# Where the operands of the products lie in the on-chip memory

## The chip, the cores and the metric

The kernel runs on one core of one Trainium2 chip. The metric is the device time of one execution in microseconds. The time before is the median of three runs, 3551.01 us (3549.99 to 3552.76).

## The reference

512 tokens of 1024 features go through two blocks of two layers each. A layer of the first block is: a SwiGLU feed-forward layer with 2816 hidden features, a token mixer (stick-breaking attention, gated delta rule and short convolution side by side), a second feed-forward layer, and a gated embedding; a layer norm follows each of the four. The two layers of the second block are attention layers: the first has three groups of windowed and dilated attention in eight heads, the second has grouped-query attention; both read 256 memory tokens as well, gate their heads, and add an output projection to x. Everything is float32. In short:

```
for i in range(DEPTH):
    x = layer_norm(ALPHA * x + 0.5 * swiglu(x, ffn_w_in[i, 0], ffn_w_out[i, 0]), ...)
    x = layer_norm(ALPHA * x + token_mix(x, ...), ...)
    x = layer_norm(ALPHA * x + 0.5 * swiglu(x, ffn_w_in[i, 1], ffn_w_out[i, 1]), ...)
    x = layer_norm(ALPHA * x + sigmoid(x @ w_gate + b) * (p[i] @ w_proj), ...)
# then, twice:  x = x + (attention heads * silu(gate)) @ w_out
```

## The kernel before, in words

Features lie on the 128 partitions, tokens along the free dimension, so a feature tile of all tokens is 128x512. Every dense product is made of three float32r products. `weight` (L144) brings a piece of a weight, [128, 1024] or [128, 768], into a staging tile `wst`, ScalarE casts it to its high part `whi` (L153), and VectorE or GpSimd takes the difference as the low part `wlo` (L154). The activations are split in the same way (`split`, L175): `xh` and `xl` are the parts of x, `hh` and `hl` those of the hidden features of a feed-forward layer, `mxh` and `mxl` those of the mixed heads, `Yh` and `Yl` those of the gated heads of the second block, `mem_p` those of the memory tokens. One step is then low weight times high activation, high weight times low activation, and high times high. Each TensorE product is a weight load (128 columns of the stationary operand) and a matmul that streams the moving operand, 512 or 256 columns wide.

In the first block the weights are stationary and the activations move, in `mm3` (L190), `mm3_side` and `gmm3`: results `pgu` (w_in of a feed-forward layer), `pfo` (w_out), `pmx` (projections of the mixer), `pmo` (its output), `pg` and `ppp` (the gated embedding). In the second block `mm3k` (L1151) does them. For `p_in` (projections to heads) and `p_mkv` (keys and values of the memory tokens) the activations are stationary and the weights move; for `p_gate` and `p_out` it is as in the first block. The attention itself (`att_p`, `att_o`, transposes `att_T`, `nh_t`) and the delta rule are plain float32 products between working tiles, no weights in them.

The order of the work is the order of the code, with engines waiting for each other by semaphores; the next weights are brought in while the present ones are used (two staging tiles, five pairs of parts). The change touches none of this; it touches where tiles lie.

The pools are laid one behind another along each partition in the order in which they are opened, and each tile's place is rounded up to 32 bytes. A scratch area of 16384 bytes and four constants of 32 bytes come first. Then come `const` (L116 to L128: 512 + 512 + 32 + 512 + 512 + 512 + 32 bytes), `ph` (`xh`, `xl`, 16384 bytes each), `pst` (two `wst`), `pwh` and `pwl` (five `whi`, five `wlo`, 4096 bytes each), then x or, in the second block, `mem_all`, then the small tiles of a region and its working tiles. This adds up to the following places. A tile of weights or activations within these starts a multiple of 512 bytes further on, so the remainder by 128 holds for all of them.

| tile | byte | remainder by 128 |
|---|---|---|
| `xh` / `xl` | 19136 / 35520 | 64 |
| `wst`, `whi`, `wlo` (first of each) | 51904, 60096, 80576 | 64 |
| x, `mem_all` | 101056 | 64 |
| working tiles of the first block (`hh`, `hl`, `mxh`, `mxl`, `mem_p` of its last layer, ...) | 128960 + 2048 n | 64 |
| working tiles of the second block (`Yh`, `Yl` from 157824, `mem_p` from 126080 and 145536, q, k, v) | | 0 |

So before the change the parts of weights and activations have the same remainder in all products but two: `p_out`, and `p_mkv` in its second use (at some 3190 us).

Of the kernel before, what the change touches and what calls it, by code (L numbers as in the profile page):

```python
# [31 lines left out]


class Kern:
    def __init__(self, ctx, tc, ins, outs):
        self.tc, self.nc, self.i, self.o = tc, tc.nc, ins, outs
        self.ctx = ctx
        pool = lambda n, b, **k: ctx.enter_context(tc.tile_pool(name=n, bufs=b, **k))
        self.const = pool("const", 1)
        self.ph = pool("ph", 1)  # L40
        self.pst = pool("pst", 2)
        self.pwh = pool("pwh", 5)
        self.pwl = pool("pwl", 5)
        self.pd = pool("pd", 4, space=PSUM)
        self.pm = pool("pm", 4, space=PSUM)
        self.fence = None
        self.clock = 0
        self.looked = []
        self.table(SILU)
        self.consts()  # L50

    @contextmanager
    def region(self, **sizes):
        """Working tiles of one stretch of the program."""
# [8 lines left out]
    # ---------------------------------------------------------------- tiles  # L63
# [27 lines left out]
    def table(self, name):  # L91
        """Load the activation table of what follows, once what needed the one before is done."""
        load = self.nc.scalar.preload_act_table_set(name)
        for i in self.looked:
            self.behind([load], i)
        self.looked.clear()
        return load

    def behind(self, later, first):
        """Issue order only: the instructions later go after first on their engine."""  # L100
# [5 lines left out]
    def chain(self, seq):  # L106
        """One accumulation group over several parts of a bank: the first product opens it, the last one closes it."""
        self.behind(seq[1:], seq[0])
        for i in seq[1:-1]:
            self.behind(seq[-1:], i)  # L110

    def consts(self):
# [6 lines left out]
        self.ones = c.tile([128, 1], F, name="ones")  # L119
        nc.vector.memset(self.ones, 1.0)  # L120
        self.m128 = c.tile([128, 128], F, name="m128")
        nc.vector.memset(self.m128, 1.0 / 128)
        self.mean_r = c.tile([128, 128], FR, name="mean_r")
        nc.vector.tensor_copy(self.mean_r, self.m128)
        self.ones128 = c.tile([128, 128], F, name="ones128")
        nc.vector.memset(self.ones128, 1.0)
        self.qeps = c.tile([128, 1], F, name="qeps")
        nc.vector.memset(self.qeps, 128.0 * EPS * EPS)  # L128
# [16 lines left out]
    # ---------------------------------------------------------------- weights  # L145
    def weight(self, src, n, eng=None):
        """One piece of a weight, [128, n] in DRAM, as two float32r parts whose sum is exact."""
# [11 lines left out]
    def unit(self, src, eng=None, spare=False):  # L159
        """The exact parts of a weight [128, 1024], by tiles [128, 128]; spare: held in working tiles."""  # L160
# [18 lines left out]
    # ---------------------------------------------------------------- products  # L179
    def turn(self, out, a):  # L180
        """out = a transposed."""
# [3 lines left out]
    def mm(self, out, lhsT, rhs, start, stop):  # L185
        """A product, and its columns on the tensor engine's clock."""
# [3 lines left out]
    def mm3(self, out, pairs):  # L190
        """out += sum over pairs of (stationary hi, lo), (moving hi, lo), small products first."""
# [9 lines left out]
    def mm3_side(self, groups):  # L201
        """Several products that share their moving operands, (out, stationary parts, moving parts), one pair of each
        before the next: they start while the last moving parts are still being made."""
# [9 lines left out]
    def gmm3(self, out, pairs, step=3):  # L213
        """mm3 as a generator that yields every few products."""
# [11 lines left out]
    # ---------------------------------------------------------------- statistics  # L226
    def rsqrt(self, y, v, n):
        """y = v ** -0.5, elementwise on [128, n]."""
# [14 lines left out]
    def bcast(self, out, cols):  # L243
        """out[p, j, t] = cols[t, j] for the 128 tokens t of cols [128, n], by two exact products each."""
# [13 lines left out]
class LN:  # L258
    """Layer norm over the features of y [128, 8, 512] (feature k * 128 + p), in place, fed tile by tile."""
# [6 lines left out]
    def add(self, f, ps, tk, scale):  # L266
        """y[:, f, tk] = y[:, f, tk] + scale * ps - c, c a per-token shift near the mean; f = 0 comes first."""
# [37 lines left out]
    def begin(self, tk):  # L305
        """Statistics of the tokens tk, y less its mean."""
# [28 lines left out]
    def end(self, tk, xh=None, xl=None, lead=True):  # L335
        """Normalise the tokens tk; y becomes the layer norm, xh + xl its exact parts."""
# [19 lines left out]
def ffn(K, l, j, x, xh, xl, ln, aside=None, load=None):  # L356
    """x += 0.5 / ALPHA * swiglu(x), through ln."""
# [23 lines left out]
    if load:  # L381
        # the first tokens arrive between the first weights
# [52 lines left out]
def weave(K, chains, dense):  # L435
    """Issue the tensor engine's work of chains, each of which yields how long its next step has to wait (columns), the
    first that is ready first, and of dense, which never waits for long, in between."""
# [24 lines left out]
# waits, in columns of the tensor engine  # L462
# [10 lines left out]
def mixer(K, l, xh, xl, ln):  # L473
    """x += token_mix(x) / ALPHA, through ln."""
# [22 lines left out]
    def b3(col, n=128):  # L497
        """[128, m] -> [128, m, n], repeated along the last axis"""
        return col.unsqueeze(2).to_broadcast([128, col.shape[1], n])

    def rep(m):
        """[128, n] -> [128, NH, n], repeated along the heads"""
        return m.unsqueeze(1).to_broadcast([128, NH, m.shape[1]])

    # q, k, v: projection, causal convolution, silu; features on the partitions
    qt = [K.t2((128, NH, 128), name="gq") for _ in range(4)]
    kt = [K.t2((128, NH, 128), name="gk") for _ in range(4)]
    # x is but xh + xl now; its place serves for others
# [3 lines left out]
    def conv(j, p, tk, before=None):  # L512
        """The tokens tk of the unit j, p [128, tk] in PSUM, after the three tokens before."""
# [16 lines left out]
    # values of the stick breaking attention and gates a, b, by token tile  # L530
# [82 lines left out]
def _mixer_heads(K, l, mixed, out, places, xh, xl, ab, sv, qt, kt, vt, a_log, dt_b, norm_w, sc_w, unit, gproj, b3, rep, silus, pre):  # L613
# [26 lines left out]
    def norms(ts):  # L640
        """Keys by token for the tiles ts, and the coefficients that their norms give."""
# [34 lines left out]
    def decays(t):  # L676
        """exp of the differences of the sums of log decays within the chunks, and of those sums."""
# [10 lines left out]
    def start():  # L688
        pre[0] = K.table(LOG)

        # decays and gates, [128 tokens, tile * head]
# [52 lines left out]
    def piece(t):  # L744
# [12 lines left out]
        # U = (I + N^T)^-T by doubling blocks  # L757
# [99 lines left out]
    def tail(t, po, qsq):  # L857
        """Gated rms norm; the norm of q enters through its eps."""
# [33 lines left out]
    def stick(pair):  # L892
        """Stick breaking attention of two heads, scores with the keys on the partitions: for each head keys 0 in a tile
        and keys 1 and 3 in another, for both keys 2 in a third."""
# [65 lines left out]
    def gate():  # L960
        """silu of the gate z of the gated delta net, by token tile."""
# [13 lines left out]
    def short(i):  # L975
        """Short convolution, half i."""
# [38 lines left out]
def ple(K, l, x, xh, xl, ln, rms=None, aside=None):  # L1015
    """x += sigmoid(x @ w_gate + b) * (p @ w_proj) / ALPHA, through ln."""
# [28 lines left out]
    def some(fs, W, tk):  # L1045
        """Part of the output for the tokens tk; the first products go tile by tile of x."""
# [47 lines left out]
# -------------------------------------------------------------------- second block  # L1094
#
# Token n = 128 * c + i of the second block is token 4 * i + c of the sequence: a tile of 128 tokens is
# one residue class modulo 4, so the two dilated groups stay within a tile.
# [8 lines left out]
def by_class(a):  # L1106
    """[128, 512] in sequence order -> [128, 4, 128] in the second block's order."""
# [3 lines left out]
def by_time(a):  # L1111
    """[128, 512] in the second block's order -> [128, 128, 4] in sequence order."""
# [3 lines left out]
def row_sums(K, q, tk):  # L1116
    """[128 tokens, tiles] in PSUM: column sums of q over the tokens tk."""
# [8 lines left out]
def row_rsqrt(K, st, n, eps, name, fence=False):  # L1126
    """[128, tokens] in PSUM, the same on every partition: (st / n + eps) ** -0.5."""
# [23 lines left out]
def mm3k(K, out, pairs, step=6):  # L1151
    """Like mm3, but done with each pair before the next; yields every few products."""
# [10 lines left out]
def norm_heads(K, ps, nh, gain, rope, dst):  # L1163
    """Rms norm by head of ps [128 tokens, nh, 128], rotated, then with the features on the partitions in dst."""
# [36 lines left out]
class Pieces:  # L1201
    """[128, 8, 256] held as four tiles [128, 2, 256]."""
# [16 lines left out]
def mem_norm(K, R):  # L1219
    """R [128, 256], on every partition: the inverse rms of the memory tokens."""  # L1220
# [13 lines left out]
def mem_parts(K, l, R, tiles):  # L1234
    """The norm of the memory tokens in exact parts, held in tiles [128, 2, 256]."""
# [10 lines left out]
def mem_kv(K, l, hh, hl, mk, mv, eng=None, which=(0, 1)):  # L1246
    """Keys [128, head, 256] and values [128, tile, 4 * 128] of the memory tokens."""
# [15 lines left out]
class RMS:  # L1263
    """Rms norm over the features, x(f) [128, 512] being feature tile f, into xh + xl in the second block's order."""
# [5 lines left out]
    def from_time(self, tk):  # L1270
        """Sums of squares of the tokens tk, sequence order."""
# [14 lines left out]
    def scale_time(self, tk, after=None):  # L1286
        """The normalised tokens tk, still in sequence order."""
# [21 lines left out]
    def add(self, f, ps, tk):  # L1309
        """x += ps for the tokens tk, in the second block's order, and the sum of squares."""  # L1310
# [34 lines left out]
class Head:  # L1345
    """One head of attention: scores(c) gives the scores of the queries of tile c, pieces of nk * 128 columns in PSUM,
    each with a mask to add or None; values(kt) the values of key tile kt, a list by query tile where each sees
    another; done(o) takes the result [128 features, 512] in PSUM."""
# [6 lines left out]
    def soft(self, cp):  # L1355
        """Softmax of the queries of two tiles."""
# [26 lines left out]
    def mix(self, cp):  # L1383
        """Their values."""
# [29 lines left out]
def attend(heads, ahead=0):  # L1414
    """The heads in turn; softmaxes run ahead of the values by so many pairs of tiles."""
# [21 lines left out]
def project(K, xh, xl, W, n, evac):  # L1437
    """Projection by tiles of 128 tokens: evac(c, PSUM [128, n])."""
# [13 lines left out]
class Slab:  # L1452
    """Feature tiles [128, 512] kept two to a tile."""
# [23 lines left out]
def gates(K, l, es, xh, xl, O, Y):  # L1477
    """y = o * silu(gate), in exact parts, for the feature tiles es."""
# [443 lines left out]
```

## Time and profile before

| | |
|---|---|
| median of the runs | 3551.01 us |
| span of the profiled execution, from the first to the last instruction | 3551.5 us (0.5 us above the median; the page gives no time around it) |
| TensorE, matmuls | 3410.5 us busy, 96%, 17964 of them |
| TensorE, weight loads | 2898.7 us busy, 82% |
| VectorE / ScalarE / GpSimd | 1944.7 us (55%) / 1248.1 us (35%) / 721.7 us (20%) |
| mean granted clock of TensorE | 0.975 |
| DMA | 294.40 MB, mean 83 GB/s |

A matmul's busy time contains its way through the array, so that matmuls overlap in the records; what one of them costs in a dense stretch is the distance between two starts, read from the timeline.

### The profile page before, as it was taken

To read this page: it belongs to the slowest core of one execution; us is meant where nothing else is said; L and a number is where in the kernel's file an instruction comes from. 1 tells how busy PE (TensorE), PEld (TensorE's weight loads), DVE (VectorE), ACT (ScalarE), POOL (GpSimd) and SP (SyncE) were. 2 spreads that over 40 slices of the span, in tenths; PEclk is the share of its full clock that TensorE was granted. 3 is DMA by queue.
4 is the path that set the end of the run, shared out by engine and by line. 5 is a ranking of instruction groups with operands and counts; after the bars stand their busy time and mean duration, and the time that the engine had idled before them with its cause. 6 is when DMAs were issued, how large, how long until landed. Compare 5 with 4: busy or idle time off the path is not lost. (4 is left out here: it accounts for less than half of the span.)

```text
span 3551.5 us, 46067 instructions
## 1 busy us (share of the span) xinstructions
PE 3410.5 (96%) x17964; PEld 2898.7 (82%) x17964; DVE 1944.7 (55%) x4167; ACT 1248.1 (35%) x2104; POOL 721.7 (20%) x560
## 2 busy tenths in 40 slices
PE   8999899999999799998999999987999999999998
PEld 7888887788887788888978888876888888887777
DVE  3333665663334733346565533368767767549665
ACT  3322435332223332224353322244333333334332
POOL 0002313450012500123234200234122212111100
PEclk9999999999999899999999999997999999999999
DMA  4323211123232133232111232323322222233112
GB/s 154 109 86 98 78 37 54 36 79 103 98 92 87 48 107 98 86 92 69 45 39 54 86 99 92 94 95 111 102 75 74 75 85 73 75 127 118 56 46 79
DMA packets 91657, 294.40 MB, mean 83 GB/s; under 512 B 14256, under 2 KB 16944, under 8 KB 91312
## 3 DMA queue, kind: packets, MB, share of 16 engines
q1 hardware_dynamic: 91440, 291.47, 26.0%
q8 instruction: 141, 2.31, 0.3%
q14 instruction: 76, 0.62, 0.1%
HBM read 283.96 MB, written 7.47 MB: 82 GB/s over the span
## 5 line engine op out<-in xcount | busy, mean ns | idle before, releaser
L154 DVE TENSOR_TENSOR wlo<-wst,whi 128x1024 fp32r<-128x1024 f32 (+1 forms) x403 | 479.8, 1191 | 728.2 <-ACT whi L153 725.1
L153 ACT CAST whi<-wst 128x1024 fp32r<-128x1024 f32 (+1 forms) x520 | 531.3, 1024 | 874.0 <-issue 276.0
L188 PE MATMUL pgu<-xh,wlo 128*128 128x512 f32 (+1 forms) x1504 | 568.4, 378 | 0.2 <-ACT silu L374 0.2
L188 PE MATMUL pgu<-xl,whi 128*128 128x512 f32 (+1 forms) x1504 | 564.5, 378 | 0.0
L154 POOL TENSOR_TENSOR wlo<-wst,whi 128x1024 fp32r<-128x1024 f32 x117 | 280.4, 2401 | 609.2 <-ACT whi L153 597.6
L188 PE MATMUL pgu<-xh,whi 128*128 128x512 f32 (+1 forms) x1504 | 384.9, 379 | 11.4 <-ACT xh L176 8.9
L188 PEld LDWEIGHTS pgu<-xh,whi 128*128 128x128 f32 x1504 | 287.0, 191 | 62.8 <-ACT xh L176 8.9
L188 PEld LDWEIGHTS pgu<-xh,wlo 128*128 128x128 f32 x1504 | 287.3, 191 | 51.8 <-ACT silu L374 0.6
L188 PEld LDWEIGHTS pgu<-xl,whi 128*128 128x128 f32 x1504 | 284.7, 190 | 51.8 <-DVE xl L177 0.8
L1157 PE MATMUL p_in<-whi,xl 128*128 128x512 f32 (+1 forms) x800 | 304.9, 383 | 5.9 <-DVE xl L1307 4.5
L1157 PE MATMUL p_in<-wlo,xh 128*128 128x512 f32 (+1 forms) x800 | 305.7, 382 | 0.0
L1157 PE MATMUL p_in<-whi,xh 128*128 128x512 f32 (+1 forms) x800 | 305.2, 382 | 0.0
L285 POOL TENSOR_TENSOR x<-x,ln_c 128x256 f32<-128x256 f32 (+1 forms) x84 | 96.2, 1178 | 969.4 <-ACT ln_c L282 969.4
L188 PE MATMUL pfo<-hl,whi 128*128 128x512 f32 (+1 forms) x792 | 282.7, 366 | 0.0
L188 PE MATMUL pfo<-hh,wlo 128*128 128x512 f32 (+1 forms) x792 | 282.3, 365 | 0.0
L375 DVE TENSOR_TENSOR silu<-silu,pgu 128x512 f32<-128x512 f32 (+1 forms) x94 | 61.4, 653 | 224.9 <-PE pgu L188 190.7
L188 PE MATMUL pmx<-xl,whi 128*128 128x512 f32 (+1 forms) x480 | 182.4, 383 | 0.0
L1157 PEld LDWEIGHTS p_in<-whi,xl 128*128 128x128 f32 x800 | 151.6, 189 | 34.0 <-DVE xl L1307 4.7
L188 PE MATMUL pmx<-xh,wlo 128*128 128x512 f32 (+1 forms) x480 | 179.2, 374 | 0.0
L1157 PEld LDWEIGHTS p_in<-wlo,xh 128*128 128x128 f32 x800 | 151.6, 190 | 27.7 <-issue 2.6
L1157 PEld LDWEIGHTS p_in<-whi,xh 128*128 128x128 f32 x800 | 151.5, 189 | 27.5 <-issue 2.4
L188 PEld LDWEIGHTS pfo<-hh,wlo 128*128 128x128 f32 x792 | 149.4, 189 | 24.2
(376 smaller groups left out, 6463.1 us busy)
## 6 DMA issues: line engine op xcount, KB each, us to landing
wst<-in_ffn_w_in SPq DMA_DIRECT2D x176, 512.0 KB, 3.4
wst<-in_ffn_w_out SPq DMA_DIRECT2D x64, 512.0 KB, 3.5
wst<-in_wa_qk SPq DMA_DIRECT2D x48, 512.0 KB, 3.4
wst<-in_ffn_w_out SPq DMA_DIRECT2D x32, 384.0 KB, 3.2
wst<-in_mix_w_qkv SPq DMA_DIRECT2D x24, 512.0 KB, 3.5
wst<-in_wa_v SPq DMA_DIRECT2D x24, 512.0 KB, 3.4
wst<-in_w_gate SPq DMA_DIRECT2D x24, 512.0 KB, 3.2
wst<-in_w_out SPq DMA_DIRECT2D x32, 384.0 KB, 3.1
```

The source lines that it names most:

```text
L153: nc.scalar.copy(hi, st)
L154: sub = (eng or nc.vector).tensor_sub(lo, st, hi.bitcast(F))
L188: return self.nc.tensor.matmul(out, lhsT=lhsT, rhs=rhs, start=start, stop=stop)
L285: nc.gpsimd.tensor_sub(self.y[:, k, tk], self.y[:, k, tk], c)
L375: nc.vector.tensor_mul(s, s, ps[1])
L1157: K.nc.tensor.matmul(out, lhsT=w, rhs=x, start=(j == 0), stop=(j == n - 1))
```

## The change

Two small tiles of 64 bytes are put into pools of their own, one between the staging tiles and the parts of the weights, one behind these. The constants are laid out anew: the two single columns share a tile of 128 bytes, and `m128` is no tile any more but another view of `mean_r`, which is now made from `ones128`. One small tile of the second block is made 64 bytes longer. Comments and docstrings are dropped too, so line numbers move.

```diff
+LINE = 32
...
         self.pst = pool("pst", 2)
+        self.off = pool("off", 1)
+        nc = self.nc
+        self.words = self.off.tile([128, LINE // 2], F, name="words")
+        nc.vector.memset(self.words, 0.0)
         self.pwh = pool("pwh", 5)
         self.pwl = pool("pwl", 5)
+        self.off2 = pool("off2", 1)
+        self.words2 = self.off2.tile([128, LINE // 2], F, name="words2")
+        nc.vector.memset(self.words2, 0.0)
...
-        self.ones = c.tile([128, 1], F, name="ones")
+        both = c.tile([128, LINE], F, name="both")
+        self.ones, self.qeps = both[:, 0:1], both[:, 1:2]
         nc.vector.memset(self.ones, 1.0)
-        self.m128 = c.tile([128, 128], F, name="m128")
-        nc.vector.memset(self.m128, 1.0 / 128)
-        self.mean_r = c.tile([128, 128], FR, name="mean_r")
-        nc.vector.tensor_copy(self.mean_r, self.m128)
+        nc.vector.memset(self.qeps, 128.0 * EPS * EPS)
         self.ones128 = c.tile([128, 128], F, name="ones128")
         nc.vector.memset(self.ones128, 1.0)
-        self.qeps = c.tile([128, 1], F, name="qeps")
-        nc.vector.memset(self.qeps, 128.0 * EPS * EPS)
+        self.mean_r = c.tile([128, 128], FR, name="mean_r")
+        nc.vector.tensor_scalar(self.mean_r, self.ones128, 1.0 / 128, None, op0=OP.mult)
+        self.m128 = self.mean_r.bitcast(F)
...
-            g = load_small(K, ins["norm_g"][1], (128, KD), "rmsg")
+            g = K.sm.tile([128, KD + LINE // 2], F, name="rmsg", tag="rmsg", bufs=1)[:, :KD]
+            nc.sync.dma_start(out=g, in_=ins["norm_g"][1])
```

By the same adding up the places become: `xh` 18688, `xl` 35072, first `wst` 51456 (all remainder 0 by 128); first `whi` 59712, first `wlo` 80192 (remainder 64); x and `mem_all` 100736, working tiles of the first block from 128640, `Yh` and `Yl` from 157568 (all remainder 0).

## Rows read from the trace of the kernel before

**Rows 1.** The page's first part: busy us (share of the span) xinstructions.

```profile
PE 3410.5 (96%) x17964; PEld 2898.7 (82%) x17964; DVE 1944.7 (55%) x4167; ACT 1248.1 (35%) x2104; POOL 721.7 (20%) x560
```

**Rows 2.** Groups of matmuls, 512 columns: shape, xcount | busy us, mean ns | idle before.

```profile
L188 PE MATMUL pgu<-xh,wlo 128*128 128x512 f32 x1312 | 511.6, 390 | 0.2 <-ACT silu L374 0.2
L1157 PE MATMUL p_in<-wlo,xh 128*128 128x512 f32 x672 | 268.8, 401 | 0.0
...
L188 PE MATMUL pfo<-hl,whi 128*128 128x512 f32 x616 | 239.7, 389 | 0.0
L188 PE MATMUL pmx<-xl,whi 128*128 128x512 f32 x352 | 145.0, 412 | 0.0
...
L1157 PE MATMUL p_gate<-xh,wlo 128*128 128x512 f32 x192 | 77.3, 403 | 0.0
```

**Rows 3.** The same view, products of 256 columns.

```profile
L188 PE MATMUL pmo<-mxl,whi 128*128 128x256 f32 x256 | 66.9, 295 | 3.7 <-DVE mxl L177 3.7
...
L188 PE MATMUL pgu<-xh,wlo 128*128 128x256 f32 x192 | 56.9, 299 | 0.0
L188 PE MATMUL pg<-xh,wlo 128*128 128x256 f32 x192 | 53.7, 292 | 1.8 <-ACT sig L1055 1.8
L188 PE MATMUL pfo<-hl,whi 128*128 128x256 f32 x176 | 43.0, 285 | 0.0
L188 PE MATMUL pmx<-xh,wlo 128*128 128x256 f32 x128 | 37.9, 299 | 0.0
L1157 PE MATMUL p_in<-wlo,xh 128*128 128x256 f32 x128 | 36.8, 288 | 0.0
```

**Rows 4.** Timeline, feed-forward w_in, 512 columns, twelve products apart: start us, us, what.

```profile
99.81 0.39 PE L188 MATMUL pgu<-xl,whi 128*128 128x512 f32 x1
...
102.53 0.39 PE L188 MATMUL pgu<-xl,whi 128*128 128x512 f32 x1
```

**Rows 5.** Timeline, feed-forward w_out, 256 columns, fifteen products apart.

```profile
358.12 0.28 PE L188 MATMUL pfo<-hh,wlo 128*128 128x256 f32 x1
...
359.92 0.28 PE L188 MATMUL pfo<-hl,whi 128*128 128x256 f32 x1
```

**Rows 6.** Timeline, output projection of the second block, 512 columns, sixteen apart.

```profile
3462.63 0.40 PE L1157 MATMUL p_out<-Yl,whi 128*128 128x512 f32 x1
...
3466.36 0.40 PE L1157 MATMUL p_out<-Yh,whi 128*128 128x512 f32 x1
```

**Rows 7.** Timeline, output projection of the second block, 256 columns, nine apart.

```profile
3522.01 0.28 PE L1157 MATMUL p_out<-Yh,whi 128*128 128x256 f32 x1
...
3523.03 0.28 PE L1157 MATMUL p_out<-Yh,whi 128*128 128x256 f32 x1
```

**Rows 8.** Timeline, second p_mkv, keys: fifteen products between these two.

```profile
3191.82 0.63 PE L1157 MATMUL p_mkv<-whi,mem_p 128*128 128x512 f32 x2
...
3195.32 0.63 PE L1157 MATMUL p_mkv<-whi,mem_p 128*128 128x512 f32 x2
```

**Rows 9.** Timeline, second p_mkv, values: sixteen products between these two.

```profile
3207.69 0.39 PE L1157 MATMUL p_mkv<-wlo,mem_p 128*128 128x512 f32 x1
...
3211.36 0.39 PE L1157 MATMUL p_mkv<-wlo,mem_p 128*128 128x512 f32 x1
```

**Rows 10.** Timeline, mixer output, 256 columns, five products apart.

```profile
743.93 0.41 PE L188 MATMUL pmo<-mxl,whi 128*128 128x256 f32 x1
...
745.00 1.91 PE L188 MATMUL pmo<-mxh,whi 128*128 128x256 f32 x8
```

**Rows 11.** Windows, that stretch: busy us by engine, PEclk, DMA share, GB/s.

```profile
744.00:746.00 2.00, 2.00 (x11) 2.00 (x11) 2.00 (x5) 0.42 (x1) 0.00 (x0) 0.50 0.63 229
```

**Rows 12.** VectorE groups that take the low parts: xcount | busy us, mean ns.

```profile
L154 DVE TENSOR_TENSOR wlo<-wst,whi 128x1024 fp32r<-128x1024 f32 x339 | 417.9, 1233 | 494.3 <-ACT whi L153 491.3 <-PE p_in L1157 0.9 <-PE p_gate L1157 0.4
L177 DVE TENSOR_TENSOR hl<-silu,hh 128x512 fp32r<-128x512 f32 x82 | 56.2, 686 | 4.1 <-ACT hh L176 4.1
...
L177 DVE TENSOR_TENSOR Yl<-gated,Yh 128x512 fp32r<-128x512 f32 x12 | 8.2, 684 | 0.7 <-ACT Yh L176 0.7
```

## The prediction, made before the changed kernel was seen

> **What bounds the kernel now.** I read the page's first part, then the groups of matmuls by shape, and then the timeline of single stretches. The first part says that TensorE's matmuls are busy 96% of the span, VectorE 55%, ScalarE 35%, GpSimd 20% [rows 1]. So nearly all of the time is the distance from one matmul to the next, and a change that only moves addresses can act at one place of weight: that distance. It has to be read from the timeline, because the mean of a row (390 ns for a product of 512 columns [rows 2]) contains the way through the array.
>
> In the feed-forward layer, with all weights at hand, twelve products of 512 columns take 102.53 - 99.81 = 2.72 us, 226.7 ns each [rows 4]. Products of 256 columns take (359.92 - 358.12) / 15 = 120.0 ns [rows 5]. What would they take without any loss? At the lower granted clock of 0.5 (1.2 GHz of the two levels), 256 columns take (745.00 - 743.93) / 5 = 214 ns [rows 10, 11], which is a column per cycle: 256 / 1.2 = 213.3. A column per cycle at 2.4 GHz would be 213.3 ns for 512 and 106.7 ns for 256. So at the full clock each product loses 13.4 ns (32 cycles) in either width, and at the half clock it loses none. Something is read too slowly only when TensorE runs fast; it is neither a semaphore nor a DMA, as the two starts lie in stretches without a gap.
>
> **A comparison that lies in the trace already.** Of all products with weights, two have their operands where the change puts them all, one at a multiple of 128 bytes and the other 64 bytes past one: `p_out`, whose `Yh` and `Yl` have remainder 0 and whose weights have 64, and the second `p_mkv`, with `mem_p` at 0 and weights at 64. They keep other distances than the rest:
> - `p_out`, 256 columns: (3523.03 - 3522.01) / 9 = 113.3 ns [rows 7] against 120.0. That is a gain of 6.7 ns, 16 cycles.
> - `p_out`, 512 columns: (3466.36 - 3462.63) / 16 = 233.1 ns [rows 6] against 226.7. That is a loss of 6.4 ns, again 16 cycles.
> - the second `p_mkv`, 512 columns, weights moving and activations stationary: (3195.32 - 3191.82) / 15 = 233.3 ns for the keys [rows 8], and (3211.36 - 3207.69) / 16 = 229.4 ns for the values [rows 9].
>
> So with unlike remainders the narrow products run faster and the wide ones slower, whichever of the operands moves. The wide ones know two rhythms, 233 and 229; each was kept over a whole stretch, so which one a stretch has seems to depend on how it was entered.
>
> **The change part by part.**
> - *Products of 512 columns in the two feed-forward stages.* `pgu` has 3 x 1312 = 3936 and `pfo` 3 x 616 = 1848 of them, 5784 in all; of the three products of a step one row stands [rows 2], the others have the same count. They form long dense streams like those of rows 4. Bounds for each: +2.7 ns (229.4) and +6.6 ns (233.3). I take the upper one, as `p_out` has the same roles (weights stationary at 64, activations moving at 0) and it showed 233: 5784 x 6.6 = +38 us.
> - *Products of 512 columns mixed with short ones.* `p_in` 3 x 672 = 2016, `p_gate` 3 x 192 = 576, `pmx` 3 x 352 = 1056, together 3648. Their means are 401 to 412 ns against 390 [rows 2]: attention and delta-rule products between them disturb the rhythm and they pay some of the loss today. Bounds 0 and +6.6 ns; I take half, +3.3: 3648 x 3.3 = +12 us. The few left (`ppp`, the first `p_mkv`) are under 300 products, below 2 us.
> - *Products of 256 columns.* Six kinds, three products each: 3 x (256 + 192 + 192 + 176 + 128 + 128) = 3216 [rows 3]. Each goes from 120.0 to 113.3: 3216 x -6.7 = -21.5 us. Bounds: -21.5 and 0 (the gain is lost where a narrow product waits for its operands anyway or runs at the half clock).
> - *What stays.* `p_out` and the second `p_mkv` keep unlike remainders. The float32 products of the attention have both operands among working tiles, which move together, and contain no weights. Value projections of the first block and the spare weights of its last gated embedding hold their weights in working tiles and move together with `xh` and `xl`: no change.
> - *VectorE, ScalarE, GpSimd.* Their operands move too. Taking a low part of 512 columns lasts 686 ns with all operands at 64 and 684 ns with all at 0 [rows 12]; unlike ones, as `wst` and `whi` become, no row here shows apart from others. If each `wlo` of 1233 ns became 10% longer or shorter, 339 x 0.12 = 42 us would come or go on an engine that has 45% of the span free [rows 1, 12], and the next weights are split while TensorE works on the present ones; without that cover it would be 42 us either way. Taken: 0, by the two equal rows.
> - *The constants.* One memset and a copy less, two memsets of 16 columns and a multiply more, on VectorE at the start, while the first weights are on their way: 0. No instruction is moved past a queue, and no wait is added.
>
> Sum: 38 + 12 - 21.5 = +28.5 us on the profiled execution's 3551.5, which is 0.5 us above the median; on the median this gives 3579.5, say 3580 us. The lower end, 229.4 throughout and nothing in mixed stretches, is 5784 x 2.7 - 21.5 = -6 us. The upper end, +6.6 everywhere and the full gain on narrow products, is 9432 x 6.6 - 21.5 = +41 us; with narrow products that gain nothing, +62 us.
>
> **The rivals.**
> 1. *The other rhythm.* The streams settle at 229 and not at 233. For it: the values of `p_mkv` did [rows 9]. Against it: these have the roles exchanged, and the stretches of `p_out` keep 233 [rows 6]. Time: 3551 - 6 to 3551 + 6, about 3549; the sign of its difference is open.
> 2. *The wide products gain as the narrow ones do.* If operands in different halves of 128 bytes never meet, a dense stream would lose 16 cycles less in either width: 9432 x -6.7 - 21.5 = -85 us, 3466 us. For it: the narrow products [rows 7], and that 32 cycles lost at like remainders are 16 there. Against it: no product of 512 columns in the trace does it, and those with unlike remainders do the opposite [rows 6, 8].
> 3. *Addresses are not the cause.* `p_out` and `p_mkv` differ from the rest in more than the remainder (another stage, other pools). Then nothing changes: 3551 us. Against it: `p_in`, in the same block and written by the same function but with like remainders, has means that lie with the first block's (288 ns at 256 columns, against 285 to 299 there [rows 3]), while every stretch shown with unlike remainders deviates [rows 6 to 9]. The Trainium skill, "SBUF — State Buffer", section "Who interferes with whom", has this as its rule: "PE and ACT never wait on anyone", with two independent read ports for the moving operand and the weight load. By that rule the time stays at 3551. The trace does not agree with it as it stands, since equal products keep 120.0 and 113.3 ns [rows 5, 7] and neither is a column per cycle.
>
> **How the numbers follow.** A difference over 0.2%, 7 us, can be told from no change. Forecast (slower, +7 to +62 us): 0.62. First rival: 0.15, of which two thirds within 0.2%, the rest shared. Second: 0.13. Third: 0.10. Slower: 0.62 + 0.03 = 0.65. Within 0.2%: 0.10 + 0.10 = 0.20. Faster: 0.13 + 0.02 = 0.15. The predicted time is 3580 us. The range is to hold the forecast, the first and the third rival: 3540 to 3603. The upper end is 52 us above the median, between the two upper sums. The second rival is left out, as is what lies above. The forecast's own range is 3558 to 3603.
>
> **What would show it right or wrong.** In the changed kernel's timeline the distance of `pgu` and `pfo` of 512 columns should be 233 ns and that of 256 columns 113 ns; `p_out` should stay at 233 and 113. TensorE's idle time and the counts of its groups should stay as they are, and the difference should lie mostly in the four feed-forward stages. A distance of 229 there makes the first rival right, one of 220 the second, one of 227 the third. If VectorE's or ScalarE's rows grow by a tenth and TensorE begins to wait for `wlo`, my zero for them was wrong.

## The result and the profile after

The changed kernel takes 3585.01 us (median of four runs, 3576.35 to 3587.90) against 3551.89 us (median of four runs of the kernel before): a ratio of 1.0089, 95% interval 1.0077 to 1.0101. It is slower by 33 us; 28.5 us were forecast.

First the page's first part after the change, which answers to [rows 1].

```profile
PE 3443.6 (96%) x17964; PEld 2892.9 (81%) x17964; DVE 1940.9 (54%) x4168; ACT 1243.9 (35%) x2104; POOL 721.8 (20%) x560
```

The span went from 3551.5 to 3585.3 us, by 33.8 us, and the matmuls' busy time by 3443.6 - 3410.5 = 33.1 us. TensorE's idle time is the same (141.0 and 141.7 us), the counts too, and the other engines are no busier. So the time lies between matmul and matmul. Which of them, the groups by shape say (xcount | busy us, mean ns of one), in answer to [rows 2, 3]:

```profile
L196 PE MATMUL pgu<-xh,wlo 128*128 128x512 f32 x1312 | 519.1, 396 | 0.2 <-ACT silu L382 0.2
L1165 PE MATMUL p_in<-wlo,xh 128*128 128x512 f32 x672 | 269.4, 401 | 0.0
L196 PE MATMUL pfo<-hl,whi 128*128 128x512 f32 x616 | 241.2, 392 | 0.0
...
L196 PE MATMUL pgu<-xh,wlo 128*128 128x256 f32 x192 | 55.5, 292 | 0.0
...
L196 PE MATMUL pfo<-hl,whi 128*128 128x256 f32 x176 | 42.3, 281 | 0.0
```

`pgu` of 512 columns grew by 6 ns, `pfo` by 3, `p_in` by none; the narrow ones of `pgu` and `pfo` shrank by 7 and 4. These means contain the way through the array, so the distance between starts decides. In the timeline (start us, us, what) this is the feed-forward w_in, sixteen products from the first row to the last, as [rows 4]:

```profile
99.22 0.40 PE L196 MATMUL pgu<-xl,whi 128*128 128x512 f32 x1
...
102.95 0.40 PE L196 MATMUL pgu<-xl,whi 128*128 128x512 f32 x1
```

It gives 3.73 / 16 = 233.1 ns, the forecast's rhythm. Feed-forward w_out of 512 columns (27 products, 22 of them in the first row) and of 256 columns (15 products, as [rows 5]), and the output projection of 256 columns (11 products, as [rows 7]):

```profile
345.80 5.20 PE L196 MATMUL pfo<-hh,whi 128*128 128x512 f32 x22
...
351.98 0.39 PE L196 MATMUL pfo<-hl,whi 128*128 128x512 f32 x1
...
366.88 0.28 PE L196 MATMUL pfo<-hh,wlo 128*128 128x256 f32 x1
...
368.65 0.28 PE L196 MATMUL pfo<-hl,whi 128*128 128x256 f32 x1
...
3556.80 0.28 PE L1165 MATMUL p_out<-Yh,wlo 128*128 128x256 f32 x1
...
3558.10 0.28 PE L1165 MATMUL p_out<-Yh,whi 128*128 128x256 f32 x1
```

These are 6.18 / 27 = 228.9 ns, 1.77 / 15 = 118.0 ns and 1.30 / 11 = 118.2 ns. None of the three is what I wrote down: `pfo` of 512 columns runs in the rhythm of the first rival, its narrow products gain 2 ns and not 6.7, and `p_out`, which was to stay at 113.3 ns, got slower. The remainders by 128 are as the change set them in all of these, so the remainder by 128 cannot be the whole rule.

Taking the places modulo 256 instead of 128 shows a candidate. In the changed kernel the weights lie 64 bytes past a multiple of 256, `xh` and `xl` at a multiple, but `hh`, `hl`, `Yh`, `Yl` 128 bytes past one. So the distance moving minus stationary is -64 for `pgu` and +64 for `pfo`. In the kernel before it was 0 for both, and -64 for `p_out`, which now has +64.

### The profile page after: what moved, and what is told of

It reads as the page before. It is cut to its first block, busy times and chain, and to the rows that moved or that the text cites. A ratio compares the mean times of both kernels' runs of the same rounds, so it can differ in the third digit from the quotient of the medians.

```text
span 3585.3 us, 46068 instructions
## 1 busy us (share of the span) xinstructions
PE 3443.6 (96%) x17964; PEld 2892.9 (81%) x17964; DVE 1940.9 (54%) x4168; ACT 1243.9 (35%) x2104; POOL 721.8 (20%) x560
## 4 chain that ended last, share of the span: by engine, by line
PE 85%; DVE 9%; issue 3%; ACT 2%; DMA 1%; POOL 1%; SPq 0%; DVEq 0%; ACTq 0%; POOLq 0%
PE pgu L196 27%; PE p_in L1165 14%; PE pfo L196 13%; PE pmx L196 5%; PE p_gate L1165 4%; PE p_out L1165 3%; PE pmo L196 2%; PE att_o L1412 2%; PE p_mkv L1165 1%; PE att_T L191 1%; PE pg L196 1%; PE pU L196 1%; PE pZ L196 1%; PE nh_t L191 1%; PE att_p L1577 1%
## 5 line engine op out<-in xcount | busy, mean ns | idle before, releaser
L196 PE MATMUL pgu<-xl,whi 128*128 128x512 f32 (+1 forms) x1504 | 573.1, 384 | 0.1
L196 PEld LDWEIGHTS pfo<-hh,wlo 128*128 128x128 f32 x792 | 148.7, 188 | 25.6
```

What stands on the lines that cost most here:

```text
L196: return self.nc.tensor.matmul(out, lhsT=lhsT, rhs=rhs, start=start, stop=stop)
```

## The experiments

The three layouts below that are whole kernels are compared with 3554.35 us, the median of thirteen runs of the kernel before that were made beside them. The theory, called D in the expectations: the distance moving minus stationary, modulo 256 and with its sign, sets the rhythm. Rival E: like or unlike remainders by 128, with the entry into a stretch choosing between 229 and 233. Rival A: each operand's own alignment.

**A sweep by 32 bytes.** A program of products alone, between one stationary and one moving tile whose starts have the same remainder by 256:

```diff
+order = [(w, s, m) for w in (512, 256) for s in range(8) for m in range(8)]
+for turn, seq in (("x", order), ("y", order[::-1])):
+    for w, s, m in seq:
+        p = pd.tile([128, 512], F, ...)
+        for k in range(40):
+            nc.tensor.matmul(p[:, :w], lhsT=W[:, 8 * s + k % 8 * 128:8 * s + k % 8 * 128 + 128],
+                             rhs=M[:, 8 * m + k % 4 * 512:8 * m + k % 4 * 512 + w], start=(k == 0), stop=(k == 39))
```

> This kernel has nothing of the model: it makes 40 float32r products in a row, weight load and matmul, for each pair of byte offsets of the stationary and the moving operand (0 to 224 by 32), 512 and 256 columns wide, all pairs once forward and once backward. Theory D (what counts is the distance moving minus stationary, taken modulo 256, with its sign): the distance between two starts is the same along each diagonal of the table; 0 gives 226.7 and 120.0 ns (512 and 256 columns), -64 gives 233.3 and 113.3 ns, +64 gives 229 and 117.8 ns, 128 is open. Rival A (each operand's own alignment counts): rows or columns of the table are alike, not diagonals. Rival E (like or unlike remainders by 128 count, and how a stretch was entered picks the rhythm): 0 and 128 are alike, 226.7 and 120.0; +64 and -64 are alike, each 229 or 233 by chance, and differ between the forward and the backward pass.

Measured, from the starts of the last 25 products of each 40, in ns; 16 stretches stand behind each number (eight pairs of offsets, twice):

```
distance      0      32     64     96     128    160    192    224
512 columns   226.7  233.3  228.9  233.3  232.9  234.4  233.3  233.3
256 columns   120.0  117.4  117.8  120.0  118.7  117.7  116.1  118.3
```

At 512 columns the 16 stretches of a distance agree within 0.3 ns, those of 128 within 1.2; with one operand kept in its place and the other moved, the spacing goes through all these values. So theory D holds there and rival A falls. Of rival E the remainder by 128 falls: 0 and 128 are not alike, +64 and -64 (192) are not alike. Its other half, the entry, does not fall: at 256 columns the 16 stretches at 192 keep either 113.3 ns (six of them) or 117.8 ns (ten), where theory D expected 113.3 for all.

**All remainders alike, at a multiple of 256.** The changed kernel without the two small tiles:

```diff
-        self.off = pool("off", 1)
-        self.words = self.off.tile([128, LINE // 2], F, name="words")
-        nc.vector.memset(self.words, 0.0)
...
-        self.off2 = pool("off2", 1)
-        self.words2 = self.off2.tile([128, LINE // 2], F, name="words2")
-        nc.vector.memset(self.words2, 0.0)
```

> The changed kernel without its two small tiles ahead of and behind the parts of the weights: activations stay at a multiple of 128, the parts of the weights come to one too, and every distance is 0 modulo 256, that of the output projection of the second block and of the second memory projection too. Theory D: 226.7 and 120.0 ns everywhere, 3551 us plus p_out's change (288 x -6.6 + 576 x 6.7 ns = +2 us), 3550 to 3556 us. Rival A (the activations' move to a multiple of 128 costs the time): it stays near 3585 us. Rival E: as theory D.

Measured: 3555.64 us against 3554.35, a ratio of 1.0004, interval 0.9995 to 1.0014. In its timeline the feed-forward w_in (eleven products between the rows) and the output projection of 256 columns (ten products):

```profile
99.19 0.39 PE L190 MATMUL pgu<-xl,whi 128*128 128x512 f32 x1
...
101.68 1.52 PE L190 MATMUL pgu<-xh,whi 128*128 128x512 f32 x6
...
3520.93 0.28 PE L1159 MATMUL p_out<-Yl,whi 128*128 128x256 f32 x1
...
3522.13 0.28 PE L1159 MATMUL p_out<-Yh,whi 128*128 128x256 f32 x1
```

They give 2.49 / 11 = 226.4 ns and 1.20 / 10 = 120.0 ns. With `xh`, `xl` and the constants as in the changed kernel, the time is that of before: the loss comes from the two small tiles, which set weights and activations apart, and from nothing else in the change. `p_out` of 256 columns, now at distance 0, has lost its 113.3 ns, as it must.

**The sign turned for x alone.** 128 bytes ahead of `xh`, and a longer tile behind the staging tiles so that all else keeps its place modulo 256:

```diff
+        self.off0 = pool("off0", 1)
+        self.words0 = self.off0.tile([128, 32], F, name="words0")
+        self.nc.vector.memset(self.words0, 0.0)
         self.ph = pool("ph", 1)
...
-        self.words = self.off.tile([128, LINE // 2], F, name="words")
+        self.words = self.off.tile([128, 48], F, name="words")
```

> The changed kernel with xh and xl alone 128 bytes further on (modulo 256); everything else keeps its place modulo 256. All remainders by 128 stay as in the changed kernel. Theory D: for products with xh and xl the sign of the distance turns: pgu, pmx and p_gate of 512 columns go from 233.3 to 229 ns (5568 x -4.4 = -24 us), p_in from 229.4 to 233 ns (2016 x 4 = +8 us), pgu, pg and pmx of 256 columns from 113 to 116 ns to 117.8 (1536 x 2.5 = +4 us): near 3573 us, and pfo stays at 228.9. Rival E (remainders by 128 and entry): the same as the changed kernel, 3576 to 3588 us, pgu at 233.

Measured: 3580.49 us, ratio 1.0073, interval 1.0058 to 1.0088. The feed-forward w_in (13 products between the rows) and the projections of the second block (19 products; two of the rows left out hold two each):

```profile
99.89 0.39 PE L199 MATMUL pgu<-xh,wlo 128*128 128x512 f32 x1
...
102.86 0.39 PE L199 MATMUL pgu<-xl,whi 128*128 128x512 f32 x1
...
2530.65 0.39 PE L1168 MATMUL p_in<-whi,xh 128*128 128x512 f32 x1
...
2535.08 0.40 PE L1168 MATMUL p_in<-whi,xh 128*128 128x512 f32 x1
```

2.97 / 13 = 228.5 ns and 4.43 / 19 = 233.2 ns: both turned as theory D said, with remainders by 128 that are the changed kernel's, so the remainder by 128 falls here too. The total is a miss: 3573 was expected, and the interval overlaps that of the changed kernel. The traces show where it was missed. Adding up, by kind of product, the time from each start to the next, `pgu`, `pmx` and `p_gate` of 512 columns take 22 us less than in the changed kernel (24 forecast) and `p_in` 8 us more (8 forecast). The rest came back in products whose spacing was not to change, such as `pmo` (4 us more). The clock bears on this: all four runs had a lower mean granted clock (0.971 to 0.974) than the changed kernel's four (0.975 to 0.978). For the profiled runs, 0.971 against 0.975, that is 0.004 / 0.5 x 3583 = 29 us more at the lower level, where a product of 256 columns takes 214 ns [rows 10, 11], nearly twice its time; so some 14 us are lost there, an estimate. That is of the size of the miss, but no run separates it, and why the clock lay low for longer is not shown: the rhythms bear the theory out, the total does not.

**Exceptions at +64.** The traces of the whole kernels hold stretches that the distance does not account for. In the changed kernel one stretch of `p_out`, 512 columns (30 products between the rows), and in the run with the sign turned the last stretch of `p_out`, 256 columns (28 products); both have the distance +64:

```profile
3176.12 0.40 PE L1165 MATMUL p_out<-Yh,whi 128*128 128x512 f32 x1
...
3183.11 0.39 PE L1165 MATMUL p_out<-Yh,whi 128*128 128x512 f32 x1
...
3548.77 0.28 PE L1168 MATMUL p_out<-Yl,whi 128*128 128x256 f32 x1
...
3551.94 0.28 PE L1168 MATMUL p_out<-Yh,whi 128*128 128x256 f32 x1
```

They keep 6.99 / 30 = 233.0 ns and 3.17 / 28 = 113.2 ns, where the sweep had 228.9 and 117.8 in every stretch. In the kernel before, the second `p_mkv` has the distance +64 for keys and values alike, and kept 233.3 ns for the first of them and 229.4 ns for others [rows 8, 9]. So the distance settles most of the spacing and the entry into a stretch chooses in some; what in the entry does it is open.

**Distance 128.** 128 bytes in each of the two small tiles:

```diff
-        self.words = self.off.tile([128, LINE // 2], F, name="words")
+        self.words = self.off.tile([128, 32], F, name="words")
...
-        self.words2 = self.off2.tile([128, LINE // 2], F, name="words2")
+        self.words2 = self.off2.tile([128, 32], F, name="words2")
```

> The changed kernel with 128 bytes in place of 64 in each of the two small tiles: all activations lie at a multiple of 256, all parts of the weights 128 bytes past one, so that every distance is 128 modulo 256. Rival E (remainder by 128 alone): 226.7 and 120.0 ns everywhere, 3550 to 3556 us, like the run with all at 0. Theory D: a distance that no kernel here had yet; open, between 213.3 and 233 ns for 512 columns. If the loss comes from a period of 256 bytes and half of it is the farthest apart that two operands can be, it is the smallest loss: 220 ns (16 cycles) for 512 columns, 9720 x -6.7 = -65 us, and 113 ns for 256, 3792 x -6.7 = -25 us: 3460 us.

Measured: 3599.79 us, ratio 1.0130, interval 1.0114 to 1.0147, the slowest of all layouts. Remainders by 128 are alike here, so the remainder by 128, by which 3550 to 3556 was expected, falls by the time as well. So does my guess of a smallest loss at the largest distance: in the dense stretches `pgu` keeps 233.2 ns and `pfo` 232.6 on the mean of all starts in its trace, near the 232.9 of the sweep.

**A sweep by 4 bytes.** The same program with distances from 0 to 252 by 4:

```diff
+jobs = [("s", w, 0, d) for w in (512, 256) for d in dist] + [("t", w, d, 0) for w in (512, 256) for d in dist]
+jobs += [("u", w, 0, d) for w in (256, 512) for d in reversed(dist)]
```

> Only products again, nothing of the model: 40 in a row for each distance moving minus stationary from 0 to 252 bytes by 4, 512 and 256 columns wide; first with the stationary operand fixed and the moving one shifted (names ending in s), then with the stationary one shifted back (t), then as the first in reverse order (u). The sweep by 32 bytes showed that the distance modulo 256 alone counts, with 226.7 ns at 0 as the least for 512 columns and one of two rhythms, 113.3 or 117.8 ns, at -64 for 256 columns. Theory D1 (what collides are pieces of 32 or 64 bytes): the distances within one such piece keep the same, steps show at multiples of 32 or 64, nothing is below 226.7. Rival D2 (what collides are single words): distances of a few bytes differ from 0, and some are below 226.7, down to 213.3 ns, a column per cycle. s and t agree in both.

Measured at 512 columns, ns, from the last 25 starts (the first stretch of the program, s at 0, was still settling):

```
distance                   0      4      8      16     32     64     128    192
s, moving shifted          228.9  236.7  233.3  231.7  233.3  228.9  232.1  233.3
t, stationary shifted back 226.7  226.7  233.4  228.3  233.3  228.9  233.3  233.4
u, as s, in reverse        226.7  236.7  233.3  231.7  233.3  228.9  232.3  233.4
```

Among all 192 stretches of 512 columns none is below 226.6 ns, and the highest are at 240.0. Theory D1 falls, as distances within 32 bytes do differ; D2 falls in what it hoped for, as nothing is faster than distance 0. And D itself is narrower than I had it: s and t agree at multiples of 32 bytes and not between them (236.7 and 226.7 at 4), and there the entry can choose as well (at 240, 236.7 in s and 226.7 in u).

**Shorter weight loads.** Stationary operands of 128 to 32 columns:

```diff
+for k in range(80):
+    nc.tensor.matmul(p[:c, :w], lhsT=W[:, k % 8 * 128:k % 8 * 128 + c],
+                     rhs=M[:, d // 4 + k % 4 * 512:d // 4 + k % 4 * 512 + w], start=(k == 0), stop=(k == 79))
```

> Only products, 80 in a row, with stationary operands of 128, 96, 64 and 32 columns, so that the weight load that runs beside each matmul is as long as before, three quarters, a half or a quarter of it; distances 0, 64, 128 and 192 bytes, 512 and 256 columns wide. Theory F (the loss arises while a weight load reads beside the moving operand): at 512 columns and distance 0 the loss over 213.3 ns falls with the stationary columns, about 13.4, 10, 7 and 3 ns, and the four distances come together. Rival G (the loss is a fixed price of a float32r product of this width, to which the distance adds something): it stays near 13.4 ns, and the distances keep their differences. In both, 256 columns come nearer to 106.7 ns with short weight loads.

The groups of this run by name (duration ns least/median/most, first and last start us; d is the distance, c the stationary columns):

```profile
L1734 PE MATMUL d0w512c128u<-mov,stat x80: 388/389/395, 889.6 to 907.5; 128*128 128x512 f32 x80
L1734 PE MATMUL d192w512c128u<-mov,stat x80: 394/394/395, 834.1 to 852.5; 128*128 128x512 f32 x80
L1734 PE MATMUL d0w512c32u<-mov,stat x80: 388/392/397, 668.0 to 686.3; 128*32 128x512 f32 x80
L1734 PE MATMUL d192w512c32u<-mov,stat x80: 391/394/398, 612.5 to 630.8; 128*32 128x512 f32 x80
```

Over 79 products these are 226.6, 232.9, 231.6 and 231.6 ns; the starts are rounded to 0.1 us there, and unrounded they give 226.8, 233.3, 231.5 and 231.7. Theory F falls: with a quarter of the stationary columns, whose weight load takes 108 ns in the records against 188, distance 0 is slower, not faster. The differences between distances do shrink (230.7 to 231.8 ns for the four), so rival G does not hold as written either. With 96 columns the two signs have changed places: 233.3 ns at +64 and 228.4 at 192, so the table of the sweep is one for 128 stationary columns. At 256 columns, where both expected a gain, it came: with 32 stationary columns seven of the eight stretches keep 113.3 to 113.6 ns, whatever the distance. What makes the loss is left open; that it is a read that is too slow, as the prediction has it, is not shown.

No layout that was run beats the kernel before. The one gain that the sweep points to, distance -64 for the products that are only 256 wide, needs weights 64 bytes further on in their tiles: 256 bytes more for each of ten tiles, to keep the others in step, and by my adding up of the tiles there is no room for that beside the working tiles of the first block. It was not tried.

## Why the prediction was right, and where it was not

Distances between starts, in ns, as means over runs of six products without a gap, before and after, with the counts of the prediction:

```
                  before  after   products  us
pgu 512           226.8   233.3   3936      +25.6
pfo 512           226.7   228.9   1848      +4.1
p_in 512          228.5   229.4   2016      +1.8
pmx 512           228.2   233.6   1056      +5.7
p_gate 512        228.4   233.2   576       +2.8
p_out 512         233.4   230.3   288       -0.9
pmo, pgu, pg 256  119.9   116.6   1920      -6.3
pfo 256           119.8   117.8   528       -1.1
pmx, p_in 256     119.8   116.0   768       -2.9
p_out 256         113.6   117.8   576       +2.4
```

The sum is +31.2 us of the 33.8 by which the span grew. It counts every product at the rhythm of the dense runs, and what is taken for a gap moves the means of `p_in`, `pmx` and `p_gate` by up to 1 ns. The time from each start to the next, added up by kind in the two traces with all gaps in it, gives +30.1 us for `pgu` and `pfo` of 512 columns, +6.3 for `p_in`, `pmx` and `p_gate`, -5.7 for the narrow products and +3.2 for `p_out`.

- *The bound* was right: TensorE's spacing took all of it, and the idle time stood still.
- *The comparison within the trace* was right as a method: `p_out` and the second `p_mkv` had shown that these places slow wide products and speed up narrow ones, though the remainder by 128 was not what counted.
- *Wide products of the feed-forward stages*: +38 us forecast, 25.6 + 4.1 = 29.7 measured. The term of `pgu` was right to 0.1 ns; that of `pfo` came to a third of the forecast. I had both in one role and one rhythm; by theory D their distances have opposite signs, -64 and +64. "Which one a stretch has seems to depend on how it was entered" is true of a few stretches at +64, as shown above; for `pgu` and `pfo` the sign chose, and every stretch of the sweep at +64 keeps 228.9.
- *Mixed stretches*: +12 forecast, 10.3 by the rhythms and 6.3 by the times, and not evenly: `pmx` and `p_gate` took 5 ns each, `p_in`, with the roles exchanged and so with +64, took 1. Half of the loss for each was the wrong account; it came near on the mean of the rhythms alone.
- *Narrow products*: -21.5 forecast, -10.3 by the rhythms and -5.7 by the times. I took `p_out`'s 113.3 ns for all; at +64 it is 117.8 in most stretches, and at -64 either.
- *What stays*: `p_out` did not. Its distance went from -64 to +64, +1.5 us by the rhythms. Nor did the second `p_mkv`, which went from +64 to -64 and from 229.4 ns to 233.3 for the values. The value projections and the spare weights went from 0 to 128, as `xh` and `xl` moved by 448 bytes and the working tiles by 320; they are 192 narrow products each and came to less than 1 us. The remainder by 128 hid all this.
- *VectorE, ScalarE, GpSimd and the constants at zero*: right; a `wlo` of 1024 columns took 1233 ns before and 1232 after, and the run at distance 0 throughout, with the new constants, takes the time of before.

So by the rhythms the loss was 10 us and the gain 11 us too large (14 and 16 by the times), and these nearly cancel: that the total came within 5 us is luck, and what was right in it is the cause at work, the place of the operands, and the term of `pgu`. The third rival fell: the same products kept 226.7 ns and 233.3 ns with nothing but their places changed. The rule beside it, the Trainium skill's "PE and ACT never wait on anyone" ("SBUF — State Buffer", "Who interferes with whom"), is about engines that share ports. No run here tests that; what they show is a loss that goes with the places of two operands of one engine. The second rival fell with the sweep, in which no wide product runs faster than at distance 0.

## What to carry to other kernels

In a kernel that is bound by float32r products, add up where the stationary and the moving tiles lie; moving tiles of 512 columns ran best here (with 128 stationary columns) when the distance between the two was a multiple of 256 bytes, and small tiles put between them cost up to 1.3%. A product that differs from its neighbours by 6 ns in the trace before is an experiment already made: ask in what it differs, and in more than one modulus. Two sizes that were off in opposite directions gave a good total here, so a total that fits doesn't prove its terms.

## What the runs showed that was not expected

- For products of 128 stationary and 512 moving float32r columns the spacing in the sweep depends on the distance moving minus stationary modulo 256 with its sign: 226.7 ns at 0, 228.9 at +64, 233.3 at -64, 234.4 at 160. It depends there on neither place by itself, with both at multiples of 32 bytes. In the whole kernels a few stretches at +64 keep 233 instead.
- Stretches settle into rhythms. At +64 the spacing goes 226, 229, 232 and around again, 228.9 on the mean; at 256 columns two rhythms exist at -64, and in the whole kernels at +64 too, 113.3 and 117.8 ns, and a stretch mostly keeps the one it fell into.
- A weight load of 32 columns in place of 128 made the wide products slower at distance 0, 231.5 ns against 226.8, and the narrow ones faster, 113.4 against 119.8.
